# Feed-forward: where the down phases and the transposes of the gate-up products stand in a chunk

## The chip, the core and the metric

The kernel runs on one core of a Trainium2 chip. The time is the device time of the whole program, in microseconds (us), one launch, all inputs in the chip's memory at the start. Lower is better. The chip's engines are named as the profile names them: PE (TensorE, matrix products; PEld is its weight load), DVE (VectorE), ACT (ScalarE), POOL (GpSimd), SP (SyncE, which here issues nearly all transfers).

## What is computed

Two layers of a decoder trunk on 256 rows of width 1024, in float32. Each layer has four sub-layers, each with a norm ahead and a norm behind:

```python
def swiglu(x, w_gate, w_up, w_down):
    return (jax.nn.silu(x @ w_gate) * (x @ w_up)) @ w_down

for i in range(DEPTH):                                    # DEPTH = 2
    f = swiglu(rmsnorm(h, g[0]), ffn_gate[i, 0], ffn_up[i, 0], ffn_down[i, 0])
    h = h + 0.5 * rmsnorm(f, g[1])
    mix = hybrid_mixer(rmsnorm(h, g[2]), cos_m, sin_m, cos_d, sin_d, ...)
    h = h + rmsnorm(mix, g[3])
    f = swiglu(rmsnorm(h, g[4]), ffn_gate[i, 1], ffn_up[i, 1], ffn_down[i, 1])
    h = h + 0.5 * rmsnorm(f, g[5])
    gate = jax.nn.sigmoid(rmsnorm(h, g[6]) @ w_ple_gate[i])
    h = h + rmsnorm((p[i] @ w_ple[i]) * gate, g[7])
```

The feed-forward block (`swiglu`, inner width 2816) runs four times. `cos_m`, `sin_m`, `cos_d`, `sin_d` are tables of the positions' angles, and only `hybrid_mixer` uses them.

## The kernel before

**Tiles.** The 256 rows are two row tiles, t = 0 and t = 1. The inner width of a feed-forward block is cut into six chunks, c = 0 to 5, of 512, 512, 256, 512, 512 and 512 columns. A float32 product is made of three matmuls on rounded operands: every operand x is split into `hi` (x rounded to the matmul's float32r) and `lo` (the rest), and hi·hi, lo·hi and hi·lo are summed.

**Phases of a chunk.** G0 and G1 are the gate product of row tile 0 and 1 (8 steps of three matmuls), U0 and U1 the up product, D0 and D1 the down product (8 steps too). In the narrow chunk gate and up are one phase (GU0, GU1) and a D phase has 4 steps. After G an activation writes `silu`; after U one DVE instruction writes the product `hm`. `hm` is turned by four PE transposes into `tp` (a bank of the accumulator memory); ACT then writes its hi part `hid`, DVE its lo part. D multiplies `hid` by the down weights and sums into `acc` over all chunks.

**Order of the work.** Each engine runs its instructions in the order in which the program writes them. It is written by hand: `ffn` calls the phases one after another; `run` walks a phase step by step and looks into the table `PLAN`, which has for each phase the steps at which one more weight piece is prepared (a tick) and those at which given functions are inserted (`hid_t`, the transposes and the split of `hm`, is one such function). In the chunks but the narrow one the order is G0, G1, U0, U1, D0, D1; `hid_t` of row tile 0 is inserted in U1, that of row tile 1 in D0. D1 of the narrow chunk is held back until behind G0 of the chunk that follows.

**Weights.** `Weights` streams all weights in one list, `W.add`, which has the order of use. A transfer of 1 MB brings two pieces into one of four `raw` buffers; `prepare` turns a piece into `hi` (ACT, line 159) and `lo` (DVE, line 160) in one of ten slots (eight while the mixer runs). When the second piece of a buffer is prepared, the next transfer into it is issued from SP (line 138; lines 130 for the narrow chunk, which takes gate and up columns in two transfers), so SP waits there for DVE's `lo`.

**The angle tables.** `setup_late` runs once, behind chunk 0 of the first feed-forward block. It issues four small transfers on SP (`mask`, `mult`, `freq`, `pos`; lines 303 to 306), then a chain of small DVE instructions (lines 307 to 324: `identb`, `mask`, `posf`, `ang`, `turns`, `tab`) with two ACT instructions in it (lines 319 and 323, `tab`, the sines and cosines). In the code before it is called at the end of chunk 0:

```python
            if c == 0 and not first:
                setup_late()
```

(`first` is true in the three later feed-forward blocks.)

Of the kernel before, what the change touches and what calls it, by code (L numbers as in the profile page):

```python
# [17 lines left out]
P = 128  # L18
# [32 lines left out]
}  # L51
PLAN = {
# [130 lines left out]
def hybrid_block(ctx: ExitStack, tc: tile.TileContext, a, out):  # L183
# [60 lines left out]
    for l in range(DEPTH):  # L244
        for f in range(2):
            if f == 1:
                win = a["w_in"][l].rearrange("(k p) n -> p k n", p=P)
                wo = a["w_out"][l].rearrange("(k p) n -> p k n", p=P)

                def add_in(name, c0, n):  # L250
                    for j in range(2):
                        W.add([(l, name, 2 * j), (l, name, 2 * j + 1)], win[:, 4 * j : 4 * j + 4, c0 : c0 + n], 2, n)

                add_in("A", 0, ZA)
                add_in("dq", ZA, 512)
                W.add([(l, "qu", 0), (l, "qu", 1)], a["w_q_up"][l].rearrange("(k p) n -> p k n", p=P), 1, 768)
                W.add([(l, "kvu", 0)], a["w_kv_up"][l].rearrange("(k p) n -> p k n", p=P), 1, 1024)
                add_in("dk", ZA + 512, 512)
                add_in("dv", ZA + 1024, 512)
                for half in range(2):  # L260
                    for n in range(2):
                        W.add([(l, "wo", half, n, 0), (l, "wo", half, n, 1)],
                              wo[:, 4 * half : 4 * half + 4, n * 512 : (n + 1) * 512], 2, 512)
            wg = a["ffn_gate"][l, f].rearrange("(k p) n -> p k n", p=P)
            wu = a["ffn_up"][l, f].rearrange("(k p) n -> p k n", p=P)
            wd = a["ffn_down"][l, f].rearrange("(k p) n -> p k n", p=P)
            for c, (f0, w) in enumerate(CHUNKS):
                ka = 1024 // w
                if w == 256:
                    for j in range(2):  # L270
                        W.add([(l, f, c, "GU", 2 * j), (l, f, c, "GU", 2 * j + 1)],
                              tuple(src[:, 4 * j : 4 * j + 4, f0 : f0 + w] for src in (wg, wu)), 2, 512)
                for name, src in (("G", wg), ("U", wu)) if w == 512 else ():
                    for j in range(KD // (2 * ka)):
                        W.add([(l, f, c, name, 2 * j), (l, f, c, name, 2 * j + 1)],
                              src[:, 2 * ka * j : 2 * ka * (j + 1), f0 : f0 + w], ka, w)
                for j in range(w // 256):
                    k0 = f0 // P + 2 * j
                    W.add([(l, f, c, "D", 2 * j), (l, f, c, "D", 2 * j + 1)], wd[:, k0 : k0 + 2, :], 1, 1024)
        gt = a["w_ple_gate"][l].rearrange("(k p) n -> p k n", p=P)  # L280
        for n in range(2):
            for j in range(2):
                W.add([(l, "gt", n, 2 * j), (l, "gt", n, 2 * j + 1)],
                      gt[:, 4 * j : 4 * j + 4, n * 512 : (n + 1) * 512], 2, 512)
            if n == 0:
                W.add([(l, "pe", 0), (l, "pe", 1)], a["w_ple"][l].rearrange("(k p) n -> p k n", p=P), 1, 1024)
# [49 lines left out]
    def run(gen, name, *fns):  # L336

        ticks, steps = PLAN[name]
        inserts = list(zip(steps, fns, strict=True))
        i, n = 0, 0  # L340
        for _ in gen:
            n += 1
            while i < len(inserts) and inserts[i][0] <= n:
                inserts[i][1]()
                i += 1
            if n in ticks:
                W.tick()
        for _, fn in inserts[i:]:
            fn()
# [94 lines left out]
    def ffn(l, f, pend, gain_post, gain_pre, extra=lambda: None):  # L444
# [23 lines left out]
        def up(t, c, *fns):  # L468
            w = CHUNKS[c][1]
            ps = bank("u")  # L470
            run(proj(ps[:, :w], t, gkeys(c, "U"), t == 1), f"{kind}.U{t}", *fns)
            return mul(t, ps, 0, w)
# [9 lines left out]
        def hid_t(t, hm, nblk, b0=0):  # L482
            split_t(hm, nblk, hid[t][0], hid[t][1], b0)

        def down(t, c, *fns):
            nb = CHUNKS[c][1] // P
            end = c == last
            halves = [[0], [1]] if end else [[0, 1]]

            def gen():  # L490
                for ns in halves:
                    for b in range(nb):
                        ws = W.need((l, f, c, "D", b))
                        first, final = c == 0 and b == 0, end and b == nb - 1
                        i = 0
                        for x, w in ((0, 0), (0, 1), (1, 0)):
                            for n in ns:
                                nc.tensor.matmul(accs[t][n], hid[t][x][:, b, :], ws[w][:, 0, n * 512 : (n + 1) * 512],  # L498
                                                 start=first and x + w == 0, stop=final and x == 1)
                                i += 1  # L500
                                if i % 3 == 0:
                                    if t == 1 and i == 3 * len(ns) and ns[-1] == 1:
                                        W.finish((l, f, c, "D", b))
                                    yield

            run(gen(), f"{kind}.D{t}", *fns)

        last = len(CHUNKS) - 1
        held = None
        for c, (f0, w) in enumerate(CHUNKS):  # L510
            nb = w // P
            first = c == 0 and len(pend) == 3
            kind = "start" if c == 0 and not first else "first" if first else "last" if c == last else "mid" if w == 512 else "small"
            h0 = lambda: hid_t(0, hm0, nb)
            h1 = lambda: hid_t(1, hm1, nb)
            if first:
                gate(0, c, pend[0], lo_last=True)
                hm0 = up(0, c, pend[1], pend[2])
                gate(1, c, h0)
                hm1 = up(1, c)  # L520
            elif w == 256:
                hm0 = gate_up(0, c)
                hm1 = gate_up(1, c, h0)
            else:
                gate(0, c, *(pend if c == 0 else []), lo_last=False)
                if held is not None:
                    kind = "small"
                    down(1, held)
                    held, kind = None, "mid"
                gate(1, c)  # L530
                hm0 = up(0, c)
                hm1 = up(1, c, h0)
            if c == 0:
                accs.update({t: acc(f"acc{t}") for t in range(T)})
            if c == last:
                extra()
                down(0, c, lambda: begin_post(0, accs[0], gain_post, 2.0), h1)
                xn0, half1 = post(0, accs[0], gain_post, 2.0, gain_pre)
                half1()
                down(1, c, lambda: begin_post(1, accs[1], gain_post, 2.0), lambda: x_t(0, xn0, 0))  # L540
                xn1, half1 = post(1, accs[1], gain_post, 2.0, gain_pre)
            else:
                if w == 256:
                    down(0, c)
                    h1()
                    held = c
                else:
                    down(0, c, h1)
                    down(1, c)
            if c == 0 and not first:  # L550
                setup_late()
        return pending(xn0, xn1, half1)
# [397 lines left out]
```

## Time and profile before

| | us |
|---|---|
| median of 3 runs (lowest to highest) | 1045.2 (1044.86 to 1045.64) |
| the profiled execution | 1044.43 |
| its span, first to last instruction | 1042.6 |
| PE busy | 1031.7 (99%) |
| DVE busy | 645.1 (62%) |
| ACT busy | 528.4 (51%) |
| POOL busy | 50.8 (5%) |
| mean from memory | 180 GB/s |

The numbers below the run's time come from one profiled execution. Busy time is what an engine's instructions cover; matmuls overlap in PE, so a busy PE need not be at its peak, and the distance between the starts of two matmuls tells more than their length. A timeline row has the start and the length in us, the engine, the line, the operation, what is written and read, the shapes, how many instructions the row stands for, and in brackets the idle time ahead of it and what ended it.

### The profile page before, as it was taken

To read this page: it belongs to the slowest core of one execution; us is meant where nothing else is said; L and a number is where in the kernel's file an instruction comes from. 1 tells how busy PE (TensorE), PEld (TensorE's weight loads), DVE (VectorE), ACT (ScalarE), POOL (GpSimd) and SP (SyncE) were. 2 spreads that over 40 slices of the span, in tenths; PEclk is the share of its full clock that TensorE was granted. 3 is DMA by queue.
4 is the path that set the end of the run, shared out by engine and by line. 5 is a ranking of instruction groups with operands and counts; after the bars stand their busy time and mean duration, and the time that the engine had idled before them with its cause. 6 is when DMAs were issued, how large, how long until landed. Compare 5 with 4: busy or idle time off the path is not lost.

```text
span 1042.6 us, 12658 instructions
## 1 busy us (share of the span) xinstructions
PE 1031.7 (99%) x4958; PEld 855.6 (82%) x4958; DVE 645.1 (62%) x819; ACT 528.4 (51%) x742; POOL 50.8 (5%) x123
## 2 busy tenths in 40 slices
PE   8999999999999999999999999999999999999997
PEld 5888888888888888888888888888888888888886
DVE  5764554778687554456775545557877865455474
ACT  5554443555556444344675344445564654444463
POOL 0000000200020000000110000002000200000011
PEclk9999999999999999999999999999999999999999
DMA  8864556464227554554547645455532585455601
GB/s 327 319 215 162 202 175 204 128 203 162 81 102 276 197 196 172 199 202 162 202 165 266 213 164 202 154 171 163 182 121 84 198 277 180 161 202 176 227 22 41
DMA packets 86285, 189.00 MB, mean 181 GB/s; under 512 B 3793, under 2 KB 15441, under 8 KB 86226
## 3 DMA queue, kind: packets, MB, share of 16 engines
q1 hardware_dynamic: 86082, 187.93, 52.6%
q8 instruction: 39, 0.64, 0.3%
q10 hardware_dynamic: 144, 0.26, 0.1%
q14 instruction: 20, 0.16, 0.0%
HBM read 187.13 MB, written 1.05 MB: 180 GB/s over the span
## 4 chain that ended last, share of the span: by engine, by line
PE 97%; DVE 1%; DMA 1%; ACT 0%; issue 0%; POOL 0%; SPq 0%; DVEq 0%; POOLq 0%; ACTq 0%
PE acc L498 23%; PE u L334 7%; PE u L333 7%; PE u L332 7%; PE g L332 7%; PE g L333 7%; PE g L334 7%; PE tp L409 4%; PE o L743 2%; PE sc L703 2%; PE f L332 1%; PE f L334 1%; PE f L333 1%; PE gu L334 1%; PE gu L332 1%; PE gu L333 1%
## 5 line engine op out<-in xcount | busy, mean ns | idle before, releaser
L160 DVE TENSOR_TENSOR lo<-raw,hi 128x1024 fp32r<-128x1024 f32 (+1 forms) x338 | 404.9, 1215 | 197.7 <-ACT hi L159 187.2
L159 ACT ACTIVATE hi<-raw 128x1024 fp32r<-128x1024 f32 (+1 forms) x338 | 347.2, 1049 | 167.4 <-PE u L334 79.6
L498 PE MATMUL acc<-hi,hid 128*128 128x512 f32 x704 | 201.2, 392 | 0.0
L498 PEld LDWEIGHTS acc<-hi,hid 128*128 128x128 f32 x704 | 132.2, 188 | 27.9
L332 PE MATMUL u<-hi,xh 128*128 128x512 f32 x320 | 127.0, 397 | 0.0
L333 PE MATMUL u<-lo,xh 128*128 128x512 f32 x320 | 125.0, 391 | 0.3 <-DVE lo L160 0.3
L334 PE MATMUL u<-hi,xl 128*128 128x512 f32 x320 | 125.1, 391 | 0.0
L332 PE MATMUL g<-hi,xh 128*128 128x512 f32 x296 | 116.9, 395 | 1.5 <-ACT xh L412 1.5
L498 PE MATMUL acc<-lo,hid 128*128 128x512 f32 x352 | 118.2, 395 | 0.0
L334 PE MATMUL g<-hi,xl 128*128 128x512 f32 x296 | 116.1, 392 | 0.0
L333 PE MATMUL g<-lo,xh 128*128 128x512 f32 x296 | 115.9, 392 | 0.0
L498 PEld LDWEIGHTS acc<-lo,hid 128*128 128x128 f32 x352 | 66.2, 188 | 13.1
L334 PEld LDWEIGHTS u<-hi,xl 128*128 128x128 f32 x320 | 60.1, 188 | 13.0
L333 PEld LDWEIGHTS u<-lo,xh 128*128 128x128 f32 x320 | 60.1, 188 | 12.7 <-DVE lo L160 0.6
L332 PEld LDWEIGHTS u<-hi,xh 128*128 128x128 f32 x320 | 60.1, 188 | 11.9
L412 ACT ACTIVATE hid<-tp 128x512 fp32r<-128x512 f32 (+1 forms) x48 | 27.1, 564 | 83.5 <-PE tp L409 83.5
L464 DVE SCALAR_TENSOR_TENSOR hm<-u,rs,silu 128x512 f32<-128x512 f32 x40 | 29.9, 748 | 60.7 <-PE u L334 60.5
L332 PEld LDWEIGHTS g<-hi,xh 128*128 128x128 f32 x296 | 56.0, 189 | 13.3 <-ACT xh L412 1.9
L459 ACT ACTIVATE silu<-g,rs 128x512 f32<-128x512 f32 x40 | 27.5, 688 | 77.4 <-PE g L334 77.3
L334 PEld LDWEIGHTS g<-hi,xl 128*128 128x128 f32 x296 | 55.8, 189 | 12.3 <-DVE xl L413 0.6
L333 PEld LDWEIGHTS g<-lo,xh 128*128 128x128 f32 x296 | 56.0, 189 | 12.0 <-DVE lo L160 0.5
L413 DVE TENSOR_TENSOR hid<-tp,hid 128x512 fp32r<-128x512 f32 (+1 forms) x48 | 31.1, 648 | 34.7 <-ACT hid L412 34.3
(224 smaller groups left out, 1305.7 us busy)
## 6 DMA issues: line engine op xcount, KB each, us to landing
raw<-in_ffn_down SPq DMA_DIRECT2D x44, 1024.0 KB, 5.0
raw<-in_ffn_up SPq DMA_DIRECT2D x40, 1024.0 KB, 5.2
raw<-in_ffn_gate SPq DMA_DIRECT2D x39, 1024.0 KB, 5.2
raw<-in_w_in SPq DMA_DIRECT2D x12, 1024.0 KB, 5.2
raw<-in_w_out SPq DMA_DIRECT2D x8, 1024.0 KB, 5.0
raw<-in_w_ple_gate SPq DMA_DIRECT2D x8, 1024.0 KB, 5.1
gain<-in_norm_gains SPq DMA_DIRECT2D x15, 512.0 KB, 3.8
raw<-in_ffn_gate SPq DMA_DIRECT2D x10, 512.0 KB, 4.2
```

The costliest lines, as they stand in the source:

```text
L159: self.nc.scalar.activation(hv, raw, AF.Copy)
L160: self.nc.vector.tensor_tensor(lv, raw, hv.bitcast(F32), op=ALU.subtract)
L332: nc.tensor.matmul(ps, sh, wh, start=first, stop=False)
L333: nc.tensor.matmul(ps, sh, wl, start=False, stop=False)
L334: nc.tensor.matmul(ps, sl, wh, start=False, stop=last)
L409: nc.tensor.transpose(ps[:, j * P : (j + 1) * P], src[:, (b0 + j) * P : (b0 + j + 1) * P], ident)
L412: nc.scalar.activation(hv, v, AF.Copy)
L413: nc.vector.tensor_tensor(dl[:, k0 + b0 : k0 + b0 + nb, :], v, hv.bitcast(F32), op=ALU.subtract)
L459: nc.scalar.activation(s[:, :w], ps[:, :w], AF.Silu, scale=rx[t][:, 0:1])
L464: nc.vector.scalar_tensor_tensor(hm[:, :w], ps[:, :w], rx[t][:, 0:1], sg[t][:, c0 : c0 + w], op0=ALU.mult, op1=ALU.mult)
L498: nc.tensor.matmul(accs[t][n], hid[t][x][:, b, :], ws[w][:, 0, n * 512 : (n + 1) * 512], start=first and x + w == 0, stop=final and x == 1)
L703: nc.tensor.matmul(v[:, i, :], q, k, start=False, stop=True, skip_group_check=True)
```

## The change

Three things change in the feed-forward blocks, and the rest follows from them.

1. D0 and D1 of a chunk move behind G0 of the next chunk: the order is now G0(c), D0(c-1), D1(c-1), G1(c), U0(c), U1(c). The narrow chunk has GU0, D0(c-1), D1(c-1), GU1. Only the last chunk still has its D phases at its end.
2. The transposes of both row tiles' products are inserted in one place, at step 5 of G0 of the next chunk (`turn(..., 0, 1)`), with the split of both behind them. In the last chunk they stay apart, in U1 and in D0.
3. The list of weights takes the new order of use (G of a chunk, D of the chunk before, U), and `PLAN` has new steps.

`setup_late` stands on the same line at the end of the loop over c; since D0 and D1 of chunk 0 are no longer called there, it now comes right behind U1 of chunk 0.

```diff
-    "mid.G0": ((1, 5), ()), "mid.G1": ((1, 3, 5, 7), ()), "mid.U0": ((), ()), "mid.U1": ((1, 3, 5, 7), (5,)),
+    "mid.G0": ((1,), (5,)), "mid.G1": ((1, 3, 5, 7), ()), "mid.U0": ((1,), ()),
+    "mid.U1": ((3, 5, 7), ()), "small.GU0": ((1,), (5,)), "small.GU1": ((1, 3, 5, 7), ()),
+    "inner.D0": ((), ()), "inner.D1": ((2, 4, 6, 8), ()), "last.G0": ((1,), (5,)), "last.G1": ((1, 3, 5, 7), ()),
...
+            for c, (f0, w) in enumerate(CHUNKS):
+                if w == 256:
+                    add_cols(c, "GU", (wg, wu))
+                else:
+                    add_cols(c, "G", (wg,))
+                if c:
+                    add_down(c - 1)
+                if w == 512:
+                    add_cols(c, "U", (wu,))
+            add_down(len(CHUNKS) - 1)
...
+        def turn(nb, *ts):
+            return lambda: [hid_t(t, hm[t], nb) for t in ts]
...
             if first:
                 gate(0, c, pend[0], lo_last=True)
-                hm0 = up(0, c, pend[1], pend[2])
-                gate(1, c, h0)
-                hm1 = up(1, c)
-            elif w == 256:
-                hm0 = gate_up(0, c)
-                hm1 = gate_up(1, c, h0)
+                hm[0] = up(0, c, pend[1], pend[2])
+                gate(1, c)
+                hm[1] = up(1, c)
             else:
-                gate(0, c, *(pend if c == 0 else []), lo_last=False)
-                if held is not None:
-                    kind = "small"
-                    down(1, held)
-                    held, kind = None, "mid"
-                gate(1, c)
-                hm0 = up(0, c)
-                hm1 = up(1, c, h0)
+                fns = [turn(CHUNKS[c - 1][1] // P, 0, 1)] if c else pend
+                one = gate_up if w == 256 else gate
+                new = one(0, c, *fns)
+                if c:
+                    down(0, c - 1)
+                    down(1, c - 1)
+                if w == 256:
+                    hm = {0: new, 1: gate_up(1, c)}
+                else:
+                    gate(1, c)
+                    hm[0] = up(0, c)
+                    hm[1] = up(1, c, *([turn(nb, 0)] if c == last else []))
...
-            else:
-                if w == 256:
-                    down(0, c)
-                    h1()
-                    held = c
-                else:
-                    down(0, c, h1)
-                    down(1, c)
             if c == 0 and not first:
                 setup_late()
```

**What moves on the engines**, at the joint of chunks 0 and 1 of the first block. The number behind `raw` or `acc` names the buffer's tile in the order of the program.

ACT, before, ahead of the two instructions of the angle tables (`tab`); `hi` are weight pieces, `hid` the split products of the chunk:

```order
L412 ACTIVATE hid<-tp 128x512
L159 ACTIVATE hi<-raw_263 128x1024
L159 ACTIVATE hi<-raw_285 128x1024 x2
L159 ACTIVATE hi<-raw_313 128x1024 x2
L159 ACTIVATE hi<-raw_357 128x1024
L319 ACTIVATE tab<-ang 128x2x48
L323 ACTIVATE tab<-turns 128x2x48
```

The `hid` of row tile 1 of chunk 0 (that of row tile 0 is earlier still) and six weight pieces behind it stand ahead of `tab`. ACT, with the change (`silu` is the activation of chunk 1's G0):

```order
L156 ACTIVATE hi<-raw_169 128x1024 x2
L156 ACTIVATE hi<-raw_235 128x1024 x2
L327 ACTIVATE tab<-ang 128x2x48
L331 ACTIVATE tab<-turns 128x2x48
L156 ACTIVATE hi<-raw_263 128x1024
L420 ACTIVATE hid<-tp 128x512 x2
L467 ACTIVATE silu<-g,rs 128x512
```

Both `hid` of chunk 0 now stand behind `tab` and one weight piece.

SP, before, the transfers ahead of the four small ones (`mask`, `mult`, `freq`, `pos`):

```order
L138 DMA raw_285<-in_ffn_up 128x4x512
L138 DMA raw_313<-in_ffn_up 128x4x512
L138 DMA raw_357<-in_ffn_down 128x2x1024
L138 DMA raw_386<-in_ffn_down 128x2x1024
L130 DMA raw_408<-in_ffn_gate 128x4x256
L130 DMA raw_408<-in_ffn_up 128x4x256
L130 DMA raw_431<-in_ffn_gate 128x4x256
L130 DMA raw_431<-in_ffn_up 128x4x256
L303 DMA mask_447<-in_mask 128x256
L304 DMA mult<-in_mult 128x256
L305 DMA freq<-in_freq 128x48
L306 DMA pos<-in_positions 128x2x1
```

Fourteen weight transfers are issued ahead of them, counting the narrow chunk's pairs as one. With the change:

```order
L135 DMA raw_235<-in_ffn_down 128x2x1024
L135 DMA raw_263<-in_ffn_down 128x2x1024
L135 DMA raw_285<-in_ffn_up 128x4x512
L135 DMA raw_313<-in_ffn_up 128x4x512
L127 DMA raw_335<-in_ffn_gate 128x4x256
L127 DMA raw_335<-in_ffn_up 128x4x256
L311 DMA mask_350<-in_mask 128x256
L312 DMA mult<-in_mult 128x256
L313 DMA freq<-in_freq 128x48
L314 DMA pos<-in_positions 128x2x1
```

It is eleven now: the four small ones moved ahead of three weight transfers.

DVE, before, ahead of the first instructions of the tables (`lo` are weight pieces):

```order
L413 TENSOR_TENSOR hid<-tp,hid 128x512
L160 TENSOR_TENSOR lo<-raw_263,hi 128x1024
L160 TENSOR_TENSOR lo<-raw_285,hi 128x1024 x2
L160 TENSOR_TENSOR lo<-raw_313,hi 128x1024 x2
L160 TENSOR_TENSOR lo<-raw_357,hi 128x1024
L307 CAST identb<-ident 128x128
L308 CAST mask<-mask_447 128x256
L310 CAST posf<-pos 128x2
```

Here too the second `hid` of chunk 0 and six pieces are ahead. DVE, with the change, from the last gate weights of chunk 1 (`raw_169`) on; `hm` are the products of U0 and U1 of chunk 0:

```order
L472 SCALAR_TENSOR_TENSOR hm<-u,rs,silu 128x512
L157 TENSOR_TENSOR lo<-raw_169,hi 128x1024
L157 TENSOR_TENSOR lo<-raw_235,hi 128x1024 x2
L472 SCALAR_TENSOR_TENSOR hm<-u,rs,silu 128x512
L315 CAST identb<-ident 128x128
L316 CAST mask<-mask_350 128x256
L318 CAST posf<-pos 128x2
```

The chain of the tables now starts right behind the second `hm`, and both `hid` of DVE come behind the whole chain.

More of the change, by code (lines that the diff above doesn't have):

```diff
@@ L266, in hybrid_block, with add_down @@
             wd = a["ffn_down"][l, f].rearrange("(k p) n -> p k n", p=P)
-            for c, (f0, w) in enumerate(CHUNKS):
-                ka = 1024 // w
-                if w == 256:
[L270 to L276, printed above, removed]
+            def add_down(c):
+                f0, w = CHUNKS[c]
                 for j in range(w // 256):
@@ L279, in hybrid_block, with add_cols @@
                     W.add([(l, f, c, "D", 2 * j), (l, f, c, "D", 2 * j + 1)], wd[:, k0 : k0 + 2, :], 1, 1024)
+            def add_cols(c, name, src):
+                f0, w = CHUNKS[c]
+                for j in range(2):
+                    W.add([(l, f, c, name, 2 * j), (l, f, c, name, 2 * j + 1)],
+                          tuple(v[:, 4 * j : 4 * j + 4, f0 : f0 + w] for v in src) if len(src) > 1 else
+                          src[0][:, 4 * j : 4 * j + 4, f0 : f0 + w], 2, w * len(src))
+            for c, (f0, w) in enumerate(CHUNKS):
[8 more added lines that the diff above has]
+            add_down(len(CHUNKS) - 1)
         gt = a["w_ple_gate"][l].rearrange("(k p) n -> p k n", p=P)
@@ L504, in gen @@
                                     yield
-            run(gen(), f"{kind}.D{t}", *fns)
+            run(gen(), f"{'last' if end else 'inner'}.D{t}", *fns)
         last = len(CHUNKS) - 1
-        held = None
+        hm = {}
+        def turn(nb, *ts):
+            return lambda: [hid_t(t, hm[t], nb) for t in ts]
         for c, (f0, w) in enumerate(CHUNKS):
@@ L512, in ffn @@
             first = c == 0 and len(pend) == 3
-            kind = "start" if c == 0 and not first else "first" if first else "last" if c == last else "mid" if w == 512 else "small"
-            h0 = lambda: hid_t(0, hm0, nb)
-            h1 = lambda: hid_t(1, hm1, nb)
+            kind = "first" if first else "start" if c == 0 else "last" if c == last else "mid" if w == 512 else "small"
             if first:
                 gate(0, c, pend[0], lo_last=True)
-                hm0 = up(0, c, pend[1], pend[2])
-                gate(1, c, h0)
-                hm1 = up(1, c)
-            elif w == 256:
-                hm0 = gate_up(0, c)
-                hm1 = gate_up(1, c, h0)
-            else:
-                gate(0, c, *(pend if c == 0 else []), lo_last=False)
-                if held is not None:
-                    kind = "small"
-                    down(1, held)
-                    held, kind = None, "mid"
-                gate(1, c)
-                hm0 = up(0, c)
-                hm1 = up(1, c, h0)
+                hm[0] = up(0, c, pend[1], pend[2])
+                gate(1, c)
+                hm[1] = up(1, c)
+            else:
+                fns = [turn(CHUNKS[c - 1][1] // P, 0, 1)] if c else pend
[10 more added lines that the diff above has]
+                    hm[1] = up(1, c, *([turn(nb, 0)] if c == last else []))
             if c == 0:
@@ L536, in ffn @@
                 extra()
-                down(0, c, lambda: begin_post(0, accs[0], gain_post, 2.0), h1)
+                down(0, c, lambda: begin_post(0, accs[0], gain_post, 2.0), turn(nb, 1))
                 xn0, half1 = post(0, accs[0], gain_post, 2.0, gain_pre)
@@ L541, in ffn @@
                 xn1, half1 = post(1, accs[1], gain_post, 2.0, gain_pre)
-            else:
-                if w == 256:
-                    down(0, c)
-                    h1()
-                    held = c
-                else:
-                    down(0, c, h1)
-                    down(1, c)
             if c == 0 and not first:
```

10 rows, old and new, of the table PLAN are left out of this document.

## The prediction

> **What bounds the kernel now.** I read the page first, then the waits of PE, the timeline around the first chunk, and the order of the changed program. The page's head, its first part and the chain that ended last:
>
> ```profile
> span 1042.6 us, 12658 instructions
> PE 1031.7 (99%) x4958; PEld 855.6 (82%) x4958; DVE 645.1 (62%) x819; ACT 528.4 (51%) x742; POOL 50.8 (5%) x123
> PE 97%; DVE 1%; DMA 1%; ACT 0%; issue 0%; POOL 0%; SPq 0%; DVEq 0%; POOLq 0%; ACTq 0%
> ```
>
> PE is the bound everywhere. What it waits for, all told (line waited at, releaser, us in total, times, longest):
>
> ```profile
> PE gain L889 <- DMA row<-in_norm_gains: 2.4, 1, 2.4
> PE g L332 <- ACT xh L412: 1.5, 1, 1.5
> PE u L333 <- DVE lo L160: 0.3, 1, 0.3
> ```
>
> Two of the three are the program's start, which the change leaves alone. So there are at most a few tenths of waiting to win, and the change can matter in two ways: by what a matmul stream loses around inserted transposes, and by new waits of PE. Here the stream with four transposes in it, and the end of U1 of chunk 0 in the first block (start, length, engine, line):
>
> ```profile
> 32.88 0.39 PE L334 MATMUL u<-hi,xl 128*128 128x512 f32 x1
> 33.11 0.60 PE L409 MATMUL tp<-ident,hm 128*128 128x128 f32 x4
> 33.47 0.48 PE L332 MATMUL u<-hi,xh 128*128 128x512 f32 x1
> ...
> 34.25 0.40 PE L332 MATMUL u<-hi,xh 128*128 128x512 f32 x1
> ...
> 34.71 0.39 PE L334 MATMUL u<-hi,xl 128*128 128x512 f32 x1
> 34.94 0.62 PE L498 MATMUL acc<-hi,hid 128*128 128x512 f32 x2
> 226.20 0.87 PE kmt L634 x8
> ```
>
> Matmuls start every 0.23 us (34.71, 34.94; 34.25 to 34.94 is 3 x 0.23; I reckon with 0.227, the mean over a phase), whatever their rows' lengths say. The last row is from the chain: eight transposes in 0.87 us.
>
> **The change part by part.** *Matmuls, splits, transfers.* The order holds the same instructions before and after, moved; PE's stream has the same length but for its joints. Phases of one sort following another cost nothing extra (34.71 to 34.94 is a u to acc joint of 0.23).
>
> *Transposes in one place.* From 32.88 to 34.25 stand four matmuls and four transposes: 1.37 us, less 4 x 0.227 = 0.91, so one insertion costs 0.46. Four more in the same place cost half of 0.87, 0.435. A join saves 0.46 - 0.435 = 0.03, and five chunks of four blocks have one: 20 x 0.03 = 0.6 us gained. Bounds: 0 and, were the lead-in all saved, 20 x 0.1 = 2.
>
> *`setup_late` in front of `hid`.* This is the term that decides. In the code before, the tables' chain blocks ACT and DVE for long, at no cost to PE:
>
> ```profile
> 46.37 0.37 SPq L130 DMA_DIRECT2D raw<-in_ffn_gate  x1
> 49.11 0.67 SPq L306 DMA_DIRECT2D pos<-in_positions  x1
> pos<-in_positions SPq DMA_DIRECT2D x1, 1.0 KB, 6.0
> ident<-in_ident SPq DMA_DIRECT2D x1, 64.0 KB, 3.1
> 53.99 0.29 DVE L308 CAST mask<-mask 128x256 bf16<-128x256 f32 x1 [6.35 <-DMA mask<-in_mask]
> 55.10 0.17 DVE L310 CAST posf<-pos 128x2 f32<-128x2 int32 x1 [0.82 <-DMA pos<-in_positions]
> 57.35 0.28 ACT L319 ACTIVATE tab<-ang 128x96 f32<-128x96 f32 x1 [11.11 <-DVE ang L318]
> 58.33 1.04 ACT L159 ACTIVATE hi<-raw 128x1024 fp32r<-128x1024 f32 x1
> 59.28 0.67 ACT L459 ACTIVATE silu<-g,rs 128x512 f32<-128x512 f32 x1
> 59.40 1.23 DVE L160 TENSOR_TENSOR lo<-raw,hi 128x1024 fp32r<-128x1024 f32 x1 [1.18 <-ACT hi L159]
> ```
>
> SP issues the last weight transfer pair from 46.37 on and the four small ones behind it; `pos`, 1 KB, takes 6.0 us to land behind the weights in the queue, DVE's chain runs from 55.10, and ACT, idle for 11.11 us, gets to the next weight piece only at 58.33: 58.33 - 46.37 = 11.96 us after SP began. What hid it: both `hid` of chunk 0 were done and six more pieces prepared, so PE had D0, D1 and the next G0 to run. With the change that cover is gone. ACT holds both `hid` of chunk 0 behind `tab` and one `hi`, and D0 is the first thing PE wants behind G0 of chunk 1.
>
> When does SP begin now? It needs the buffer of the seventh transfer (the first down weights), so DVE's `lo` of both its pieces:
>
> ```profile
> 24.36 2.78 SPq L138 DMA_DIRECT2D raw<-in_ffn_gate  x2
> raw<-in_ffn_gate SPq DMA_DIRECT2D x1, 1024.0 KB, 5.4
> 24.43 4.84 ACT L159 ACTIVATE hi<-raw 128x1024 fp32r<-128x1024 f32 x5
> 30.73 1.22 DVE L160 TENSOR_TENSOR lo<-raw,hi 128x1024 fp32r<-128x1024 f32 x1
> 40.58 6.92 DVE L160 TENSOR_TENSOR lo<-raw,hi 128x1024 fp32r<-128x1024 f32 x6 [0.26 <-ACT hi L159]
> ```
>
> Up to here the orders agree. The seventh transfer (24.36, 5.4 us to landing) is there at 29.8; ACT is free at 24.43 + 4.84 = 29.3 and has both `hi` by about 31.8. DVE's piece at 30.73 is the last before them; six pieces in 6.92 are 1.14 from one to the next, so the two run from 31.87 and end at 30.73 + 2 x 1.14 + 1.22 = 34.23. Before, too, SP went on right as such a piece ended (the fifth of the six: 40.58 + 4 x 1.14 + 1.22 = 46.36; SP 46.37). So SP begins at 34.23, with one 1 MB transfer (issued at about 32) ahead of the pair as before, and ACT reaches its next `hi` at 34.23 + 11.96 = 46.19. The first `hid` follows 0.95 later (58.33 to 59.28) and takes 0.60 (next fence): 47.74, and PE starts 0.05 later, 47.79.
>
> When does PE want it? U1 of chunk 0 ends without its insertion at 34.94 - 0.46 = 34.48. G0 of chunk 1 has 24 matmuls, 5.45, and eight transposes, 0.46 + 0.435: D0 is due at 40.83. **PE waits 47.79 - 40.83 = 7.0 us.** Bounds: `pos` may land up to 0.5 earlier or 1 later, since the queue then carries other row sizes; so 6.5 to 8.
>
> *`lo` of the first `hid`.* D0's fifth matmul needs it. DVE does the piece first (1.07 after ACT's `hi` starts, 58.33 to 59.40), then `hid`, 1.14 later, for 0.69: 46.19 + 2.90 = 49.09. At 0.227 the fifth matmul is due at 47.79 + 0.91 = 48.70: 0.4 us more. At half that speed it is due at 49.5 and waits for nothing.
>
> *The speed after the wait.* The trace has two restarts of PE:
>
> ```profile
> 9.61 0.80 PE L332 MATMUL g<-hi,xh 128*128 128x512 f32 x1 [1.54 <-ACT xh L412]
> ...
> 11.57 0.63 PE L332 MATMUL g<-hi,xh 128*128 128x512 f32 x1
> 12.00 0.63 PE L333 MATMUL g<-lo,xh 128*128 128x512 f32 x1
> ...
> 12.85 0.57 PE L332 MATMUL g<-hi,xh 128*128 128x512 f32 x1
> 13.26 0.40 PE L333 MATMUL g<-lo,xh 128*128 128x512 f32 x1
> 13.50 0.39 PE L334 MATMUL g<-hi,xl 128*128 128x512 f32 x1
> 531.94 0.50 PE L333 MATMUL u<-lo,xh 128*128 128x512 f32 x1 [0.30 <-DVE lo L160]
> 532.27 0.40 PE L334 MATMUL u<-hi,xl 128*128 128x512 f32 x1
> 532.50 0.39 PE L332 MATMUL u<-hi,xh 128*128 128x512 f32 x1
> 38.36 0.60 PE L409 MATMUL tp<-ident,hm 128*128 128x128 f32 x4
> 39.00 0.60 ACT L412 ACTIVATE hid<-tp 128x512 fp32r<-128x512 f32 x1 [1.81 <-PE tp L409]
> 39.63 0.69 DVE L413 TENSOR_TENSOR hid<-tp,hid 128x512 fp32r<-128x512 f32 x1
> ```
>
> (The last three rows are the `hid` that the other steps use.) At the start, behind a stretch in which PE had little to do, matmuls start 0.43 apart until 13.26, 3.65 us after the first; from there 0.23. After the short gap at 531 the spacing is 0.23 at once. A wait of 7 us is far from the 0.3 and nearest to the start, so I take the start's: 3.65 / 0.43 = 8.5 matmuls, each 0.2 late, **1.7 us**, and then no wait for `lo`. The bounds are 0 (with the 0.4 for `lo`) and 1.7, or twice that if the slow stretch is longer.
>
> The Trainium skill, page "TensorE: Matmul & The Clock Gate", section "What's actually happening", says that the array's clock falls to half after an idle window of about 3.4 us and returns after a busy one of that length. By it the sum would take the slow restart for certain, as an estimate 3.4 / 0.43 x 0.2 = 1.6 us, up to twice that where the window falls badly; without it, the full speed of 531 would be as good a guess. No row here shows the clock fall in mid-kernel.
>
> *The other 19 joints.* From the first transpose to the end of ACT's `hid` are 39.60 - 38.36 = 1.24 us, to the end of DVE's 40.32 - 38.36 = 1.96. D0 comes 0.9 (transposes) + 9 x 0.227 = 2.94 after the first transpose and needs the `lo` 0.91 later: 1.7 and 1.9 to spare. `hm` of U1 has the five steps of G0, 3.4 us, and needs 0.75 behind at most one piece. ACT has one weight piece in G0 (0.95), at step 1, so ahead of the transposes. Weight pieces: D1 and G1 now take four each in 5.45 us; DVE needs 4 x 1.14 = 4.6. Cost: nothing. The three weight transfers that SP now issues behind the four small ones are wanted only from chunk 2 on.
>
> **Sum:** 7.0 + 1.7 - 0.6 = +8.1 us. On the profiled execution (1044.43, 1.8 around its span of 1042.6) that is 1052.5; the median of the runs lies 0.8 higher, so 1045.2 + 8.1 = **1053.3 us**.
>
> **Rivals.**
> - *Full speed after the wait.* As at 531: 7.0 + 0.4 - 0.6 = +6.8, 1052.0. For it speaks that no row shows the clock fall later than the start; against it, that the wait is over twenty times that of 531.
> - *Every joint waits.* Should the piece at step 1 of G0 be held by its transfer, ACT's `hid` is held too. Four buffers leave six pieces, at least 6 x 1.14 = 6.8 us, between a transfer's issue and its use, against the 5.4 above; 0.5 us late beyond the 1.7 at each of 19 joints gives +9.5 on the 8.1: 1062.8.
> - *The small transfers land sooner.* If they passed the weights, `pos` might land as `ident` did at the program's start, in 3.1 us, 2.9 sooner; PE would wait 4.1 and restart slowly all the same: +5.2, 1050.4.
> - *Not slower.* The first joint's wait is gone if ACT reaches its `hi` by 40.83 - 1.60 = 39.2, so `pos` would have to land by 39.2 - (58.33 - 55.10) = 36.0. SP issues it 2.74 behind the pair (46.37 to 49.11), at 37.0 at the earliest. It would take a `setup_late` that isn't on the path where the order shows it; then only the joins count: 1044.6, within what can be told.
>
> **How the numbers follow.** Forecast 0.70; full speed 0.15; sooner landing 0.03; every joint 0.06; not slower 0.06, of it 0.02 for more than 0.2% (2.1 us, about what a measurement of this kernel tells from no change). So slower 0.94, same 0.04, faster 0.02. The range, 1051.0 to 1056.0, reaches from full speed with the earlier landing and half a microsecond more from the joins (1052.0 - 0.5 - 0.5) to the forecast with the later landing and a slow stretch twice as long (1053.3 + 1.0 + 1.7).
>
> **What would show it.** The waits of PE have a new row, `acc` waiting for ACT's `hid`, once, of some 7 us, at 40.8 in the timeline; ACT's idle time ahead of the first `tab` stays above 10 us but starts near 32; the next 8 or so `acc` matmuls start 0.43 apart; no other joint of the 20 has a wait; the part behind 60 us is the old one, later by 8. The prediction is wrong if PE's wait at that place is under 5 or over 9 us, if `acc` waits at other joints, or if the spacing behind the wait is 0.23 at once.

## The result and the profile after

| | before | with the change |
|---|---|---|
| median of 4 runs, us | 1045.42 (1044.86 to 1046.01) | 1052.08 (1051.52 to 1052.87) |
| ratio of times, 95% interval | | 1.0071 [1.0058, 1.0083] |
| the profiled execution, us | 1044.43 | 1051.52 |
| its span, us | 1042.6 | 1049.7 |

The change makes the kernel 0.7% slower; 1053.3 was forecast, 1051.0 to 1056.0 as the range. From the page after, the span and the first part, then the waits of PE:

```profile
span 1049.7 us, 12670 instructions
PE 1032.2 (98%) x4958; PEld 857.8 (82%) x4958; DVE 645.4 (61%) x819; ACT 532.5 (51%) x742; POOL 50.9 (5%) x123
```

```profile
PE acc L506 <- ACT hid L420: 6.5, 1, 6.5
PE gain L892 <- DMA row<-in_norm_gains: 2.4, 1, 2.4
PE g L340 <- ACT xh L420: 1.4, 1, 1.4
PE u L341 <- DVE lo L157: 0.4, 1, 0.4
```

One new row, once. The timelines of SP, DVE, ACT and PE at that place, in the order of the chain of causes (start, us, engine, line, operation; in brackets the idle time before it and what ended it):

```profile
34.57 0.37 SPq L127 DMA_DIRECT2D raw<-in_ffn_gate  x1
37.03 0.43 SPq L314 DMA_DIRECT2D pos<-in_positions  x1
42.98 0.17 DVE L318 CAST posf<-pos 128x2 f32<-128x2 int32 x1 [0.44 <-DMA pos<-in_positions]
45.23 0.28 ACT L327 ACTIVATE tab<-ang 128x96 f32<-128x96 f32 x1 [11.94 <-DVE ang L326]
46.20 1.04 ACT L156 ACTIVATE hi<-raw 128x1024 fp32r<-128x1024 f32 x1
47.15 1.06 ACT L420 ACTIVATE hid<-tp 128x512 fp32r<-128x512 f32 x2
40.85 0.39 PE L342 MATMUL g<-hi,xl 128*128 128x512 f32 x1
47.78 1.22 PE L506 MATMUL acc<-hi,hid 128*128 128x512 f32 x2 [6.54 <-ACT hid L420]
48.80 1.05 PE L506 MATMUL acc<-lo,hid 128*128 128x512 f32 x2
49.65 1.91 PE L506 MATMUL acc<-hi,hid 128*128 128x512 f32 x4
51.36 0.68 PE L506 MATMUL acc<-lo,hid 128*128 128x512 f32 x2
51.87 1.09 PE L506 MATMUL acc<-hi,hid 128*128 128x512 f32 x4
```

The transfer of `pos` in the view of the DMA issues (KB, and us from issue to landing):

```profile
pos<-in_positions SPq DMA_DIRECT2D x1, 1.0 KB, 5.9
```

G0 of chunk 1 starts its last matmul at 40.85, so D0 is due at 41.08; it starts at 47.78, 6.70 later, when ACT has done `tab`, one weight piece and the first `hid`. From 47.78 to 51.36 are eight matmuls in 3.58 us, 1.8 more than at 0.227. The wait and what follows it in the view of windows (behind the bounds and the length stand the busy times of PE, PEld, DVE, ACT and POOL; the number behind these five is the granted clock, that is, the share of its full rate at which PE was clocked):

```profile
41.08:44.60 3.52, 0.15 (x1) 0.00 (x0) 1.74 (x8) 0.00 (x0) 0.00 (x0) 1.00 0.03 7
44.60:47.78 3.18, 0.00 (x1) 0.01 (x1) 1.83 (x8) 2.05 (x5) 0.00 (x0) 0.50 0.00 0
47.78:51.42 3.64, 3.64 (x9) 2.87 (x10) 3.14 (x4) 1.96 (x3) 0.00 (x0) 0.50 0.00 0
51.42:54.84 3.42, 3.42 (x16) 2.80 (x15) 0.00 (x0) 0.00 (x0) 0.00 (x0) 1.00 0.73 221
```

PE's clock falls to half during the wait, at 44.60, and is full again from 51.42. The rest of the kernel got faster. From the first gate matmul to the end of the last down matmul, by the starts of PE's matmuls, the second, third and fourth feed-forward block take 187.38, 187.10 and 187.38 us instead of 187.78, 187.42 and 187.73: 0.3 to 0.4 less each.

### The profile page after: what moved, and what is told of

Its sections match the earlier page's. It is cut to its first block, busy times and chain, and to the rows that moved or that the text cites. A ratio compares the mean times of both kernels' runs of the same rounds, so it can differ in the third digit from the quotient of the medians.

```text
span 1049.7 us, 12670 instructions
## 1 busy us (share of the span) xinstructions
PE 1032.2 (98%) x4958; PEld 857.8 (82%) x4958; DVE 645.4 (61%) x819; ACT 532.5 (51%) x742; POOL 50.9 (5%) x123
## 4 chain that ended last, share of the span: by engine, by line
PE 93%; DVE 1%; ACT 0%; issue 0%; POOL 0%; DVEq 0%; POOLq 0%; ACTq 0%
PE acc L506 23%; PE u L341 7%; PE u L342 7%; PE u L340 7%; PE g L342 6%; PE g L340 6%; PE g L341 6%; PE tp L417 3%; PE o L746 2%; PE sc L706 2%; PE f L340 1%; PE f L342 1%; PE f L341 1%; PE gu L342 1%; PE gu L341 1%; PE gu L340 1%
## 5 line engine op out<-in xcount | busy, mean ns | idle before, releaser
L506 PE MATMUL acc<-lo,hid 128*128 128x512 f32 x352 | 114.5, 392 | 0.0
L420 ACT ACTIVATE hid<-tp 128x512 fp32r<-128x512 f32 (+1 forms) x48 | 24.8, 560 | 58.4 <-PE tp L417 58.4
```

Of the source, the lines that this page charges most:

```text
L420: nc.scalar.activation(hv, v, AF.Copy)
```

## Experiments

**1. The tables where they stood in the order.** `setup_late` is called behind D1 of chunk 0; nothing else differs from the change.

```diff
                 if c:
                     down(0, c - 1)
                     down(1, c - 1)
+                if c == 1 and l == 0 and f == 0:
+                    setup_late()
...
-            if c == 0 and not first:
-                setup_late()
```

> The changed kernel with setup_late called behind D1 of chunk 0, where it stood in the order before. My theory (the whole loss is the tables' chain ahead of the first hid, 6.7 us of waiting and 1.8 of slow restart, and the rest of the change gains 0.3 to 0.4 per feed-forward block): PE's acc never waits for hid, 1052.1 - 8.5 = 1043.6 us, 1.8 faster than before (ratio 0.998). Rival (the new order of phases itself costs, by contention or weight pieces that come late): the wait at the first joint goes, but the time stays above 1046.

Measured: 1050.29 us, ratio 1.0044 [1.0031, 1.0058]. My time did not come out. The rival's sign did, a wait that is gone at the first joint and a time above 1046, but the trace shows another cause than the rival's. The row of PE's longest wait in the view of waits:

```profile
PE tp L417 <- DVE hm L472: 4.0, 2, 3.3
```

And the timelines of ACT, DVE and PE there:

```profile
65.32 0.28 ACT L327 ACTIVATE tab<-ang 128x96 f32<-128x96 f32 x1 [10.62 <-DVE ang L326]
67.36 5.76 DVE L157 TENSOR_TENSOR lo<-raw,hi 128x1024 fp32r<-128x1024 f32 x5 [1.18 <-ACT hi L156]
73.05 0.74 DVE L472 SCALAR_TENSOR_TENSOR hm<-u,rs,silu 128x512 f32<-128x512 f32 x1
73.71 3.48 DVE L157 TENSOR_TENSOR lo<-raw,hi 128x1024 fp32r<-128x1024 f32 x3
77.11 0.74 DVE L472 SCALAR_TENSOR_TENSOR hm<-u,rs,silu 128x512 f32<-128x512 f32 x1
77.91 1.04 PE L417 MATMUL tp<-ident,hm 128*128 128x128 f32 x4 [3.34 <-DVE hm L472]
```

The wait has moved one joint on. ACT and DVE lose their 11 us behind D1 now, catch up on eight weight pieces that stand ahead of the two `hm` of chunk 1, and the transposes in the next GU0 find `hm` late, by 0.8 and 3.4 us; a slow stretch of 1.7 follows. That is 5.9 of the 6.7 us above my forecast; besides, PE's first up matmul starts at 25.34 in this execution and at 23.86 in the change's, a scatter of the program's start (see the last section). So the loss went along with the tables' chain, and this place did not show what the rest of the change costs. In the later three blocks there is no wait, and they take 187.39, 187.05 and 187.39.

**2. The transfers early, the chain where the change has it.** The four small transfers are issued at the program's start, ahead of the fifth weight transfer.

```diff
-    def setup_late():
-
+    late_in = {}
+
+    def setup_in():
         mask32 = k2("mask32")[:, : 2 * P]
+        late_in["mask32"] = mask32
         nc.sync.dma_start(mask32, a["mask"].rearrange("p c q -> p (c q)"))
         nc.sync.dma_start(mult, a["mult"])
         nc.sync.dma_start(freq, a["freq"])
         nc.sync.dma_start(pos, a["positions"].rearrange("b (t p) -> p (b t)", p=P))
+
+    setup_in()
+
+    def setup_late():
+
+        mask32 = late_in["mask32"]
...
```

> The changed kernel with the four small transfers issued at the program's start; the chain of DVE and ACT instructions stays in front of hid. My theory (of the 6.7 us nearly all is the wait for the landing, the chain itself is 3.2 us and fits under G0): ACT reaches its weight piece at about 39.5 and the first hid ends at 41.0, so PE waits 0 to 0.5 us there and does not slow down: 1044.0 us. Rival (the place of the chain in the queues is what costs, whatever the landing): a wait of 3 us or more stays, 1047 or more.

Measured: **1043.67 us, ratio 0.9987 [0.9978, 0.9996]**, faster than the change and a little faster than before, as my theory had it (1044.0); the rival's 1047 fell. The timelines of ACT, PE and DVE at the joint:

```profile
38.86 0.28 ACT L335 ACTIVATE tab<-ang 128x96 f32<-128x96 f32 x1 [4.98 <-DVE ang L334]
39.83 1.04 ACT L156 ACTIVATE hi<-raw 128x1024 fp32r<-128x1024 f32 x1
40.78 1.06 ACT L428 ACTIVATE hid<-tp 128x512 fp32r<-128x512 f32 x2
41.45 0.39 PE L350 MATMUL g<-hi,xl 128*128 128x512 f32 x1
41.67 0.62 PE L514 MATMUL acc<-hi,hid 128*128 128x512 f32 x2
42.05 1.28 DVE L429 TENSOR_TENSOR hid<-tp,hid 128x512 fp32r<-128x512 f32 x2
42.13 0.61 PE L514 MATMUL acc<-lo,hid 128*128 128x512 f32 x2
42.79 1.20 PE L514 MATMUL acc<-hi,hid 128*128 128x512 f32 x4
```

The chain stands in the same place in both queues, and PE does not wait for ACT's `hid` (41.45 to 41.67 is one matmul). It starts the fifth matmul at 42.79 and the sixth 0.34 behind, 0.3 us late in all, when DVE's first `lo` of `hid` is done. What costs is the wait for the landing that the chain brings into the queues of ACT and DVE, not the chain's own 3 us.

**3. The tables' call alone, in the kernel before.** The old order of phases and transposes, with `setup_late` ahead of D0 and D1 of chunk 0.

```diff
+            if c == 0 and not first:
+                setup_late()
             if c == 0:
                 accs.update({t: acc(f"acc{t}") for t in range(T)})
...
-            if c == 0 and not first:
-                setup_late()
```

> The kernel before, with one thing changed: setup_late is called ahead of D0 and D1 of chunk 0. The old order of phases and transposes stays. My theory (only the order of tables against hid matters): hid of row tile 1 comes behind the chain, D1 of chunk 0, due at 40.4, waits to about 45.5 and restarts slowly: 5 + 1.7 = 6.8 above before, 1052.2. Rival (it takes the moved down phases): the time of before, 1045.4, within 1.

Measured: 1052.40 us, ratio 1.0067 [1.0053, 1.0081], as much as the whole change and as my theory had it (1052.2). PE's wait in the view of waits:

```profile
PE acc L498 <- ACT hid L412: 4.6, 1, 4.6
```

The timelines of ACT and PE, then two windows, the end of the wait and the slow stretch:

```profile
42.38 0.28 ACT L319 ACTIVATE tab<-ang 128x96 f32<-128x96 f32 x1 [6.83 <-DVE ang L318]
45.25 0.57 ACT L412 ACTIVATE hid<-tp 128x512 fp32r<-128x512 f32 x1
45.88 1.22 PE L498 MATMUL acc<-hi,hid 128*128 128x512 f32 x2 [4.57 <-ACT hid L412]
45.05:45.88 0.83, 0.00 (x1) 0.00 (x1) 0.83 (x2) 0.83 (x3) 0.00 (x0) 0.50 0.00 0
45.88:51.88 6.00, 6.00 (x14) 4.71 (x15) 6.00 (x6) 4.26 (x5) 0.00 (x0) 0.50 0.83 285
```

The moved phases are not needed for the loss. The wait is shorter than in the change (4.7 by the starts, 5 expected) and the slow stretch longer: fourteen matmuls, nearly all 0.43 apart, a loss of 2.9 where I had 1.7. Experiment 6 shows why.

**4. The transposes apart again**, on the first experiment's kernel.

```diff
-                fns = [turn(CHUNKS[c - 1][1] // P, 0, 1)] if c else pend
+                fns = [turn(CHUNKS[c - 1][1] // P, 1)] if c else pend
...
-                    hm[1] = up(1, c, *([turn(nb, 0)] if c == last else []))
+                    hm[1] = up(1, c, turn(nb, 0))
```

(And alike in U1 of the first chunks and in GU1, with a step for it in `PLAN`.)

> The first experiment's kernel (tables behind D1 of chunk 0) with the transposes apart again: row tile 0's in U1 (GU1) of its own chunk, row tile 1's in G0 of the next. It undoes the join alone. My theory (the join saves 0.03 us at each of 20 places, the rest of the gain lies in the moved down phases): 0.6 above the first experiment. Rival (the whole gain of 0.35 per block is the join's): 1.4 above it. No gain from the join at all would be the third: equal.

Measured: 1052.95 us, ratio 1.0075 [1.0062, 1.0087], 2.7 above the first experiment. The time alone misleads: the first block is 2.35 longer (and its first gate matmul 0.9 sooner), since PE's wait at the second joint is one of 6.2 instead of 0.8 and 3.4:

```profile
PE tp L417 <- DVE hm L472: 6.2, 1, 6.2
```

The three undisturbed blocks tell: 187.75, 187.49 and 187.75, so 0.36 to 0.44 more than joined. All that the change gains in a block (0.3 to 0.4) is the join's, as the rival had it and not my theory: at 187.75, 187.49 and 187.75 the blocks are where they were before (187.78, 187.42 and 187.73), though the down phases stand elsewhere.

**5. The transfers one weight transfer earlier.** `setup_in` as in experiment 2, but called in U1 of chunk 0 (an inserted function at step 3), so that the four are issued ahead of the narrow chunk's pair.

```diff
-    "start.U1": ((2, 4, 6), ()),
+    "start.U1": ((2, 4, 6), (3,)),
...
-                    hm[1] = up(1, c, *([turn(nb, 0)] if c == last else []))
+                    hm[1] = up(1, c, *([turn(nb, 0)] if c == last else [setup_in] if c == 0 else []))
```

> The changed kernel with the four small transfers issued one weight transfer earlier, in U1 of chunk 0, ahead of the narrow chunk's pair; the chain stays in front of hid. My theory (the wait follows the landing one for one): pos lands some 3.3 us sooner, at about 39.7, ACT reaches its weight piece at 42.9, PE waits to 44.5 instead of 47.8: 3.4 us. The restart is slow after 3.4 too (in the first experiment a wait of 3.39 had seven slow matmuls behind it): 1052.1 - 3.3 = 1048.8. Rival (a wait as short as this one keeps the speed): 1047.2.

Measured: 1049.41 us, ratio 1.0045 [1.0028, 1.0062]. The timelines of ACT and PE:

```profile
43.33 1.04 ACT L156 ACTIVATE hi<-raw 128x1024 fp32r<-128x1024 f32 x1
44.91 0.73 PE L512 MATMUL acc<-hi,hid 128*128 128x512 f32 x2 [3.45 <-ACT hid L426]
```

ACT is free 2.9 us sooner than in the change (46.20) and PE's D0 starts 2.9 sooner (44.91): landing and wait go one for one. PE itself is 0.2 later here, so the wait is 3.6 instead of 6.7. The restart is slow here too, though it begins late: four matmuls start at full speed, and the eight gaps behind the fourth are 0.41 to 0.59; the first of them holds 0.2 of waiting for DVE's `lo` of `hid`.

**6. A ladder of waits.** On the second experiment's kernel, n activations of 0.95 us on a scratch tile ahead of `hid` in 19 joints, n from 5 to 11 (a table in the program has the n of each joint; `held` takes the place of `turn` there).

```diff
+        def held(nb, n):
+            def fn():
+                for _ in range(n):
+                    nc.scalar.activation(junk, h[0], AF.Copy)
+                turn(nb, 0, 1)()
+            return fn
```

> The second experiment's kernel (early transfers), with 5 to 11 activations that copy a row tile to a scratch tile (0.95 us each, their result is not used) put ahead of hid in 19 of the 20 joints, so that PE waits there for different times, about 0.95 n - 3.8 us: 1.0, 1.9, 2.9, 3.8, 4.8, 5.7, 6.7 for n of 5 to 11. It asks how long PE must wait to restart slowly, and for how long. Theory: waits over some 3.4 us are followed by 8 to 14 matmuls 0.43 apart (a loss of 1.7 to 2.8), shorter ones by matmuls at 0.23. Rival 1: the slow stretch grows with the wait, from the shortest on. Rival 2: any wait over 1 us brings the whole stretch. Total by the theory: waits 66 us, some 12 slow restarts 24 us, so 1135 us.

Measured: 1147.76 us in one run. By the starts of PE's matmuls, the wait and the loss in the matmuls behind it (that over 0.227 each, in those more than 0.3 apart):

| waits, us | behind them |
|---|---|
| 0.77, 1.33, 1.82, 1.86, 2.41, 2.91, 2.93 | full speed; 0.1 in the first matmul |
| 2.95 | six matmuls at full speed, then eight slow: 1.7 |
| 4.00, 4.00, 4.01, 4.04 | slow: 1.7, 1.5, 2.5, 1.7 |
| 5.09, 5.11, 5.68 | slow: 2.7, 2.3, 1.8 |
| 6.17, 6.21, 7.26, 7.85 | slow: 1.8, 2.9, 2.7, 2.8 |

The first matmuls behind a wait of 2.9 (two rows) and of 4.0, on PE's timeline:

```profile
132.41 0.73 PE L515 MATMUL acc<-hi,hid 128*128 128x512 f32 x2 [2.75 <-ACT hid L429]
132.98 0.63 PE L515 MATMUL acc<-lo,hid 128*128 128x512 f32 x2
170.17 1.22 PE L515 MATMUL acc<-hi,hid 128*128 128x512 f32 x2 [3.84 <-ACT hid L429]
171.19 1.05 PE L515 MATMUL acc<-lo,hid 128*128 128x512 f32 x2
```

The windows behind these two, then the part behind the wait of 2.95 ahead of the clock's fall and that behind it (granted clock behind the five engines):

```profile
132.41:134.40 1.99, 1.99 (x9) 1.64 (x10) 1.27 (x2) 1.02 (x2) 0.00 (x0) 1.00 0.00 0
170.17:175.40 5.23, 5.23 (x13) 4.12 (x14) 1.27 (x2) 1.01 (x2) 0.00 (x0) 0.51 0.00 0
603.84:605.33 1.49, 1.49 (x6) 1.24 (x7) 1.27 (x2) 1.02 (x2) 0.00 (x0) 1.00 0.00 0
605.33:608.74 3.41, 3.41 (x9) 2.63 (x8) 0.00 (x0) 0.00 (x0) 0.00 (x0) 0.50 0.02 5
```

Both rivals fell: none of the seven waits up to 2.93 us slows PE, all from 3.39 (the first experiment's) on do, and what a slow stretch costs, 1.5 to 2.9, does not grow with the wait. The theory came out but for the wait of 2.95, which is below its 3.4. Ten of the 13 us that the sum lies above the expected are longer waits (76 us by the starts, not 66).

The record of the granted clock in the traces shows what decides instead. In all eight traces every stretch between two changes of the clock is a whole multiple of 3.413 us: the half-speed ones last 3.41, 6.83 or 10.24, the full-speed ones for example 30.72 in the change and 153.60 first in the ladder. Counted from its first change, the time falls into windows of 3.413 us. A window at full speed in which PE stood idle (from 0.227 behind a matmul's start to the next start) for 2.2 us or more always ended with a fall, one with under 1.9 never did; of the two between, one of 1.92 did and one of 2.06 did not. The wait of 2.95 had 1.92 in one window, and the clock fell at its end, at 605.33, when PE was at work again; the wait of 2.91 was cut 1.38 and 1.53 by the bound of two windows, and nothing fell. The clock came back at the end of the first window in which PE had stood idle for under 0.8 us, and stayed down with more than 1. What PE loses is the half-speed time that is left when its wait ends: 3.64 us in the change (47.78 to 51.42), 6.00 in experiment 3 (45.88 to 51.88), though both times the clock was down for 6.83.

## Why the prediction was right

*The wait at the first joint.* Forecast 7.0 (40.83 to 47.79), measured 6.70 (41.08 to 47.78). SP began 0.34 later than worked out and the landing of `pos` was 5.9 instead of 6.0; the start of D0 hit to 0.01, in part because small errors cancelled, and PE itself came 0.25 later. That the tables' place, and nothing else in the change, brings it, experiments 2 and 3 show from both sides.

*The slow restart.* Forecast 1.7, measured 1.8. The row chosen, the program's start, was the right neighbour, and the one at 531 the wrong one. The Trainium skill, page "TensorE: Matmul & The Clock Gate", section "What's actually happening", has the clock halve after an idle window of about 3.4 us that runs free of the kernel. The traces agree on the window, 3.413 us, and on its running free; it need not be idle throughout, as 1.92 us in one window were enough in the ladder. That the size came out was chance: it depends on where in a window the wait ends, and experiment 3 lost 2.9 behind a shorter wait. The row that gave the size was chance too: the slow start that lasted 3.65 us in the trace before lasts up to 6.7 in the others (see the last section).

*`lo` of `hid`.* With the slow restart it was to cost nothing, and PE has no wait for it in the change. At full speed, in experiment 2, it cost 0.3, near the 0.4 of the rival.

*The joins.* Forecast -0.6, measured -1.4 (6.70 + 1.8 against the span's +7.1). This term was mis-sized by more than a factor of two. My step took three matmuls behind the transposes and stopped there. Followed over twelve, an insertion of four transposes costs 0.49 us, since the matmuls stay a few ns late for long, and one of eight still 0.89: a join of two saves 0.09, not 0.03. Experiment 4 puts about the same number on it, 0.36 to 0.44 for five joins. Of the 1.0 us by which the span grew less than the forecast 8.1, 0.8 are this term and 0.3 the shorter wait; 0.1 more of slow restart goes against them.

*The other joints.* None waits, as said. But the margin there is used up when ACT and DVE come late: the first experiment's chain, which held ACT until 65.32, still made the transposes of 73.94 and 77.91 late.

*The rivals.* Full speed fell with the window of clock 0.50. Earlier landing was tried by making it so (experiments 2 and 5): in experiment 5 PE's start came sooner by as much as the landing, and in experiment 2 the wait was gone. Not slower would have needed `pos` by 36.0; it was issued at 37.03.

## What to carry to other kernels

Where a helper that waits for a transfer is called at the end of a loop body, a change of that body moves the helper in every engine's queue: look for what stands behind it there, and issue its transfers long before, so that no queue holds the wait. A stall that costs nothing is hidden by work that can be named; a new order is to be searched for the places where that work is gone. On PE, where it bounds the kernel, price a wait of 3.4 us or more with the slow restart behind it, here 1.5 to 2.9 us more; for one of 2 to 3.4 us the traces leave it to where the clock's window falls.

## What the runs showed of the hardware

Three things that I had not expected. The clock may fall when PE is at work again: behind 2.95 us of waiting six matmuls ran at full speed (granted clock 1.00 from 603.84 to 605.33) and the next eight at half (0.50 to 608.74). An insertion of four transposes is felt for some ten matmuls: 0.46 us over the first three, 0.49 over twelve.

Last, the same program start is not equally fast: PE's matmuls stay 0.43 apart for 3.6 us behind the first gate matmul in the trace before and for 6.7 in the first experiment's, and from there to the first up matmul PE takes 13.98 and 15.45 us. (The view of windows gives a clock of 1.00 there, as the trace's record of the clock begins with its first change, at 13.23 before; the distance of the matmuls decides.) So up to 1.5 us of difference between two traces can lie ahead of all that the change moved.
